# First stage of a two-layer diffusion block: small vectors as columns, band means by token tile, pool weights amid conditioning

## The chip, the cores and the metric

The kernel runs on one core of a Trainium2 chip, in one launch. The metric is the time of the device for one execution, in microseconds, as the median of the runs of one kernel. A profile of a single execution goes with it: its span runs from the first to the last instruction. Engine names in the profile: PE is TensorE's matmuls, PEld its weight loads, DVE is VectorE, ACT is ScalarE, POOL is GpSimd, SP is SyncE, which issues the loads and stores (DMA).

## The reference

Two layers run over 512 latent tokens and 256 context tokens of width 1024, all in float32. Layer 0 mixes tokens by pooling, layer 1 by attention; each is followed by a squared-ReLU MLP. What matters here is the start of layer 0:

```python
sh1, sc1, gt1, sh2, sc2, gt2 = ada_mods(c, w_ada[i], b_ada[i])       # silu(c) @ w + b, six vectors of 1024
csh1, csc1, cgt1, csh2, csc2, cgt2 = ada_mods(c_ctx, w_ada[i], b_ada[i])
h_lat = modulate(rms_norm(x, g_mix_pre[i]), sh1, sc1)                # h * (1 + scale) + shift
y_lat = pool_mixer(h_lat, w_pool[j], pool_scale[j])                  # per group of 256 channels:
                                                                     # (mean over 2, 4, 8 or 16 tokens - h) @ w_pool[g]
x = x + gt1 * rms_norm(y_lat, g_mix_post[i])
m_lat = sq_relu_mlp(modulate(rms_norm(x, g_mlp_pre[i]), sh2, sc2), w_mlp_in[i], w_mlp_out[i])
x = x + gt2 * rms_norm(m_lat, g_mlp_post[i])
```

The context goes the same way with its own vectors. The output is the latent stream after both layers.

## The kernel before

**Tiling.** Tokens come in six tiles of 128 (`NL` = 4 latent, then 2 context, `NT` = 6), channels in eight tiles of 128 (`KT` = 8, index k). A weight matmul in full precision is made of three in the format float32r (high by high, high by low, low by high), for which weights and activations are split: a cast on ACT (`split`, L128) and a subtraction on DVE (L131). The matmuls of the bands, the conditioning, the gate rows and the transposes take plain float32; each of them shows as two instructions in the profile.

**Order.** The work of a stage is put into a list of steps, each with a time that serves as a rank (`st.at(t, fn, ...)`, class `Steps`), and is emitted in the order of these ranks. A planner then places the emitted instructions on the engines by its own timeline: what is ready by that timeline may go ahead of what was emitted earlier. Only instructions marked with `keep_in_program_order` stay as emitted; the loads of `raw_load` are such. All loads and stores are issued by SP in one queue.

**First stage** (steps at L713 to L751). Its parts, with the lines that the profile names:

- Small vectors (L185 to L214). `b_ada`, the gains, `c` and `c_ctx` are loaded as rows of 128 into two work tiles `pr1` and `pr2`, between the loads of x; two transposes on TensorE (L208, L209) turn them into columns in the PSUM tile `pp`. From there come the conditioning input `cond` (SiLU on ACT, L211), `cols` (L213) and `gpc` (L214).
- x (`xload`, L191). Six loads of 512 KB, the pooling bands (`band`) after the third.
- `rows_a`, `rows_b`. Per token tile: square and sum on ACT (L156), two small operations on POOL (L163, L171), scaling on DVE into `acc` (L332).
- Bands. Pooling is a matmul of the token tile with a band matrix of 144 columns; `bands` is made from the loaded one by four copies on DVE (L401, L402). `mean_mm(k, narrow)` (L420) does all six token tiles of one channel tile into a PSUM buffer (`psm`): of the pool `psA`, which has two buffers of two banks, or, for k = 4 and 7, two of `psB`, which has four of one bank. For k = 0 and 1 `mean_ev` (L434) moves the result to `stage` in SBUF.
- Conditioning (`ada_mm`, `ada_sel`). Fourteen blocks in the order of `CONDITIONING` (scale and shift before the mixer, gate, scale and shift before the MLP), twenty loads of 1 MB through a ring of four buffers (`rawe`). Each load takes matmuls (L226), a block then a DVE transpose (L228), small matmuls (L233) and one to three small DVE operations (L244 to L253). The buffer of a load comes free when these have read it.
- `centred(k)` applies scale and shift to the means of channel tile k and splits the result: three operations on ACT (L452, L455) and three on DVE (L454, L456).
- `pool_weights`. One load through the same ring, the pool scale as a broadcast load, a product on DVE (L469), then the split on ACT and DVE.
- `pool_a(t)` (L480) is the pool matmul of a token tile, 24 instructions into one buffer of `psA`. It needs every `centred` and the pool weights. Then come its mean square on ACT, the gate (`gate_rows`, L302 and L304, out of the seventh and eighth conditioning blocks), residual, norm, transposes (`turn0`, L378), modulation (`mod0`) and the first products of the MLP (`part`, L553), tile pair by tile pair.

The rank lines that the change touches are these:

```python
    landing = (21, 26.3, 29, 32, 39, 42, 47.3, 52.6, 61, 66, 69, 72, 74.8, 77.7)
    for z, (m, j, w) in zip(landing, CONDITIONING):
        ada_at(st, z, 0, m, j, w)
    for k in range(KT):
        st.at([15, 16, 18, 20, 22, 29.5, 31, 35][k], mean_mm, k, k in (4, 7))
        if k < 2:
            st.at(16.5 + k, mean_ev, k, (True, False))
        st.at([27.5, 28.5, 29.6, 30.6, 33.2, 34.2, 43.2, 44.2][k], centred, k)
    st.at(33.5, pool_weights)
```

After the first stage the MLP of layer 0, attention and the MLP of layer 1 follow, with their own steps; the first matmul of the next block is L553 with the tile `units`.

## Time and profile before

| | |
|---|---|
| median of 3 runs | 1178.87 us (1178.73 to 1179.42) |
| profiled execution | 1180.54 us, span 1178.7 us |
| PE busy | 1142.6 us, 97% |
| DVE busy | 941.9 us, 80% |
| ACT busy | 637.5 us, 54% |
| first stage | 0 to 109.9 us |

A row of the timeline gives start and duration in us, engine, line, operation, the tiles written and read, the shape and the count, and in brackets the idle time ahead of it with what ended it. A row of the table by stretches gives busy time and instructions of each engine, then the clock granted to TensorE, the busy share of the DMA engines and their rate. A row of groups gives the count, the busy time in us, the mean of one in ns, and the idle time ahead with what ended it. DMA issues are listed with the size and the time from issue to landing.

### The profile page before, as it was taken

What the parts mean: (1) busy time and instruction counts of PE and PEld (TensorE: products, weight loads), DVE (VectorE), ACT (ScalarE), POOL (GpSimd) and SP (SyncE); (2) the same over time, 40 slices, a digit from 0 to 9 for tenths busy, and PEclk for the clock granted to TensorE, in tenths of its full rate; (3) what the DMA queues carried; (4) which work ended last, traced back from release to release, by engine and by line L of the source; (5) the groups of instructions that cost most, each with busy time, mean ns of one, the idle gap of its engine ahead of it and who ended that gap; (6) DMA issues with size and microseconds to landing.
All of it is one profiled execution on the core that took longest, in us unless ns stands there. A gap on an engine that the chain in (4) does not pass through costs nothing.

```text
span 1178.7 us, 15984 instructions
## 1 busy us (share of the span) xinstructions
PE 1142.6 (97%) x6170; PEld 989.5 (84%) x6170; DVE 941.9 (80%) x1546; ACT 637.5 (54%) x1087; POOL 67.2 (6%) x120
## 2 busy tenths in 40 slices
PE   5899999999999999999999999999899999999997
PEld 4679888989889988998887889998888888888886
DVE  3786778998988999896787689877687779778876
ACT  3666654555354445554676377863676346535522
POOL 2030000000000000000141210001100000000001
PEclk9899999999999999999999999999999999999999
DMA  8974222333334334334422101115234124304312
GB/s 325 369 290 196 72 72 107 143 143 144 143 143 142 113 139 143 107 132 151 182 72 75 70 1 36 37 43 199 110 119 174 48 97 142 108 36 143 107 38 105
DMA packets 25642, 147.84 MB, mean 125 GB/s; under 512 B 2736, under 2 KB 5216, under 8 KB 9824
## 3 DMA queue, kind: packets, MB, share of 16 engines
q1 hardware_dynamic: 25568, 146.84, 34.1%
q8 instruction: 48, 0.79, 0.3%
q14 instruction: 26, 0.21, 0.1%
HBM read 139.49 MB, written 7.34 MB: 125 GB/s over the span
## 4 chain that ended last, share of the span: by engine, by line
PE 54%; issue 33%; DVE 5%; ACT 3%; POOL 3%; DMA 1%; SPq 0%; POOLq 0%; DVEq 0%; ACTq 0%
PE pso L771 22%; PE psin L677 18%; PE psin L553 3%; PE po L1230 2%; PE psy L1256 2%; PE psq L1018 2%; PE pss L1191 2%; POOL rs L171 1%; PE psada L226 1%; PE psm L420 1%; POOL rs L1027 1%; ACT junk L156 1%; DVE sm L1195 1%; PE pspt L1216 1%; DVE units L1219 1%
## 5 line engine op out<-in xcount | busy, mean ns | idle before, releaser
L771 PE MATMUL pso<-units,rb 128*128 128x512 f32 x1152 | 278.9, 392 | 0.0
L771 PEld LDWEIGHTS pso<-units,rb 128*128 128x128 f32 x1152 | 214.7, 188 | 41.1
L268 DVE SCALAR_TENSOR_TENSOR rows<-raw,cond,rows 128x256 f32<-128x256 f32 x280 | 127.1, 479 | 2.0
L783 DVE TENSOR_TENSOR acc<-acc,pso 128x512 f32<-128x512 f32 x129 | 85.4, 677 | 41.8 <-PE pso L771 41.7
L553 PE MATMUL psin<-ra,rb 128*128 128x512 f32 (+1 forms) x432 | 104.8, 342 | 2.4 <-ACT ra L363 1.6
L875 PE MATMUL pso<-units,pairs 128*128 128x512 f32 x336 | 82.3, 389 | 0.0
L553 PEld LDWEIGHTS psin<-ra,rb 128*128 128x128 f32 x432 | 70.3, 189 | 13.7 <-ACT ra L363 1.9
L553 PE MATMUL psin<-ra 128*128 128x512 f32 x256 | 80.5, 389 | 0.0
L875 PEld LDWEIGHTS pso<-units,pairs 128*128 128x128 f32 x336 | 63.1, 188 | 13.1
L879 DVE TENSOR_TENSOR acc<-acc,pso 128x512 f32<-128x512 f32 x72 | 48.8, 683 | 28.6 <-PE pso L875 28.6
L169 POOL TENSOR_SCALAR ms<-ss 128x1 f32<-128x1 f32 x20 | 11.0, 549 | 1000.7 <-ACT junk L156 989.2
L677 PE MATMUL psin<-ra,units 128*128 128x384 f32 x336 | 65.5, 337 | 0.4 <-ACT psin L689 0.4
L677 PE MATMUL psin<-sums,units 128*128 128x384 f32 x336 | 64.0, 336 | 0.0
L677 PEld LDWEIGHTS psin<-ra,units 128*128 128x128 f32 x336 | 59.8, 188 | 3.9 <-ACT psin L689 0.5
L131 DVE TENSOR_TENSOR units<-raw,units 128x1024 fp32r<-128x1024 f32 (+2 forms) x49 | 55.2, 1153 | 6.5 <-ACT units L128 6.3
L677 PEld LDWEIGHTS psin<-sums,units 128*128 128x128 f32 x336 | 58.9, 188 | 1.6
L128 ACT CAST units<-raw 128x1024 fp32r<-128x1024 f32 (+2 forms) x49 | 46.9, 995 | 17.7 <-PE pso L771 13.7
L553 PEld LDWEIGHTS psin<-ra 128*128 128x128 f32 x256 | 48.1, 188 | 10.0
L781 ACT COPY acc<-pso 128x512 f32<-128x512 f32 x48 | 27.1, 587 | 48.2 <-PE pso L771 47.7
L553 PE MATMUL psin<-rb 128*128 128x512 f32 (+1 forms) x144 | 52.8, 367 | 0.2 <-DVE rb L364 0.2
L1018 PE MATMUL psq<-units,ra 128*128 128x512 f32 x216 | 51.7, 392 | 0.0
L553 PE MATMUL psin<-rb,ra 128*128 128x512 f32 x128 | 49.8, 389 | 0.0
(255 smaller groups left out, 2355.7 us busy)
## 6 DMA issues: line engine op xcount, KB each, us to landing
raw<-in_w_ada SPq DMA_DIRECT2D x48, 1024.0 KB, 4.9
raw<-in_w_mlp_in SPq DMA_DIRECT2D x32, 1024.0 KB, 4.8
raw<-in_w_mlp_out SPq DMA_DIRECT2D x32, 1024.0 KB, 5.0
raw<-in_w_qkv SPq DMA_DIRECT2D x6, 1024.0 KB, 4.8
spill<-xr SPq DMA_DIRECT2D x10, 512.0 KB, 9.1
xr<-spill SPq DMA_DIRECT2D x10, 512.0 KB, 5.6
raw<-in_w_o SPq DMA_DIRECT2D x4, 1024.0 KB, 4.9
xr<-in_x SPq DMA_DIRECT2D x4, 512.0 KB, 4.4
```

Of the source, the lines that this page charges most:

```text
L128: a = sc.copy(hi, raw)
L131: b = ve.tensor_tensor(out=lo, in0=raw, in1=hi, op=ALU.subtract)
L268: ve.scalar_tensor_tensor(out=r, in0=raw[:, k, :], scalar=cond[:, k, c:c + 1], in1=r, op0=ALU.mult, op1=ALU.add)
L553: te.matmul(ps[:, bank, o:o + ln], w[:, k, fs], rhs, start=start, stop=(k == KT - 1 and n == 2), skip_group_check=len(ks) < KT)
L677: te.matmul(bank, w[k], a[k], start=start and k == 0 and m == 0, stop=stop and k == 3 and m == 2, skip_group_check=True)
L771: te.matmul(pss[h][:, 0:cols[h][1]], a[:, f, ts_], w[:, f, cols[h][0]:sum(cols[h])], start=(n == 0 and not seeded[t]), stop=(n == len(seq) ...
L781: sc.copy(d, ps)
L783: ve.tensor_tensor(out=d, in0=d, in1=ps[:, 0:w], op=ALU.add)
L875: te.matmul(ps, a, w, start=(m == 0), stop=(m == len(seq) - 1))
L879: ve.tensor_tensor(out=M[n][:, t], in0=M[n][:, t], in1=ps, op=ALU.add)
L1018: te.matmul(ps, a[:, k, sl], w[:, k % 4, :], start=(k == 0 and n == 0), stop=(k == KT - 1 and n == 2))
L1191: te.matmul(ps[:, c2, 0:384], a[:, sl], b[:, kv, 384 * c2:384 * c2 + 384], start=(n == 0), stop=(n == 2))
```

## The change

The host packs the small vectors as columns into one array `vecs` of 128 by 176; two loads ahead of x bring them in, the seven loads of rows, the two transposes and the copies from PSUM go. SiLU reads its input from `phase`. The bands' load follows the first tile of x. Bands are worked by token tile: `band_open` takes the PSUM buffers of a pair of channel tiles (latent means in `psA`, context means of both in one buffer of `psB`), `band_mm(t, ks)` does one token tile for several channel tiles, `band_ev` moves the pairs of k = 0 and k = 2 to `stage`. The first four channel tiles are done as the token tiles come, the others later, one k at a time. The pool weights are loaded after the fourth conditioning load (step 21.5; before, after the sixth, step 33.5). The ranks of the other steps of this stage are moved, the first block's load of MLP weights behind one more conditioning block.

```diff
@@ -79,8 +78,8 @@
 
     acc = const.tile([P, NT * D], F32, name="acc")
     ident = const.tile([P, P], F32, name="ident")
-    cols = const.tile([P, 128], F32, name="cols")
-    gpc = const.tile([P, 32], F32, name="gpc")
+    vec = const.tile([P, 160], F32, name="vec")
+    cols, gpc = vec[:, 0:128], vec[:, 128:160]
     cond = const.tile([P, KT, 32], F32, name="cond")
     sel = const.tile([P, 32], F32, name="sel")
     mods = [const.tile([P, 48, 2], F32, name=f"mods{i}") for i in range(2)]
@@ -182,36 +181,19 @@
     ve.memset(cond, 0.0)
     ve.tensor_scalar(out=onesr, in0=ident[:, 0:2], scalar1=0.0, scalar2=1.0, op0=ALU.mult, op1=ALU.add)
 
-    pr1 = work_tile()[:, 0:P]
-    pr2 = work_tile()[:, 0:P]
-    ve.memset(pr2, 0.0)
-    row = lambda a: a.rearrange("l (r p) -> (l r) p", p=P)
+    given = phase[:, 16:32]
+    sy.dma_start(given, vecs[:, 160:176])
+    sy.dma_start(vec, vecs[:, 0:160])
     xt = x.rearrange("b (t p) d -> p (b t) d", p=P)
     ct = ctx_in.rearrange("b (t p) d -> p (b t) d", p=P)
     xload = lambda t: sy.dma_start(xr[:, t, :], xt[:, t, :] if t < NL else ct[:, t - NL, :])
     xload(0)
-    sy.dma_start(pr2[32:40, :], row(c))
-    sy.dma_start(pr2[40:48, :], c_ctx.rearrange("(r p) -> r p", p=P))
-    xload(1)
-    sy.dma_start(pr2[0:16, :], row(g_mix_post))
-    sy.dma_start(pr2[16:32, :], row(g_mlp_post))
-    xload(2)
     sy.dma_start(gate.rearrange("p a n -> p (a n)")[:, 8 * BW:12 * BW + 64], band)
-    xload(3)
-    sy.dma_start(pr1[0:96, :], row(b_ada))
-    sy.dma_start(pr1[96:112, :], row(g_mix_pre))
-    xload(4)
-    sy.dma_start(pr1[112:128, :], row(g_mlp_pre))
-    xload(5)
-
-    pp = psB.tile([P, 512], F32, tag="b", name="pp")
-    te.transpose(pp[:, 128:256], pr2, ident)
-    te.transpose(pp[:, 0:128], pr1, ident)
+    for t in range(1, NT):
+        xload(t)
+    sc.activation(cond[:, :, 0:2].rearrange("p k c -> p c k"), given.rearrange("p (c k) -> p c k", k=KT),
+                  AF.Silu)
     ve.tensor_reduce(out=sel, in_=ident.rearrange("p (j c) -> p c j", c=32), axis=AX.X, op=ALU.add)
-    sc.activation(cond[:, :, 0:2].rearrange("p k c -> p c k"),
-                  pp[:, 160:176].rearrange("p (c k) -> p c k", k=KT), AF.Silu)
-    ve.tensor_copy(cols, pp[:, 0:128])
-    ve.tensor_copy(gpc, pp[:, 128:160])
 
     rowsd, parts, seeded, stale = {}, {}, {}, [0]
 
@@ -401,38 +383,33 @@
         ve.tensor_copy(bands[:, v], bands[:, 2])
         ve.tensor_copy(bands[:, v, :, c:c + HALO], edges[:, v])
 
-    means = {}
-
-    def mean_mm(k, narrow):
-        g = k // 2
-        if narrow:
-            ps = [psB.tile([P, 512], F32, tag="b", name="psm") for _ in range(2)]
-        else:
-            both = psA.tile([P, 2, 512], F32, tag="a", name="psm")
-            ps = [both[:, q, :] for q in range(2)]
-        means[k] = ps
-        for q, n in ((0, NL), (1, NT - NL)):
-            for i in range(n):
-                v = 0 if i == 0 else (1 if i == n - 1 else 2)
-                lo = max(i * P - HALO, 0)
-                hi = min((i + 1) * P + HALO, n * P)
-                c0 = lo - (i * P - HALO)
-                te.matmul(ps[q][:, lo:hi], accv[:, q * NL + i, k * P:(k + 1) * P],
-                          bands[:, v, g, c0:c0 + hi - lo], start=(i == 0), stop=(i == n - 1),
-                          skip_group_check=True)
-
-    stage = []
-
-    def mean_ev(k, on_act):
-        if len(stage) % 2 == 0:
-            stage.append(rawp.tile([P, 2048], F32, tag="raw", name="stage"))
-            d = stage[-1][:, 0:TOK]
-        else:
-            stage.append(stage[-1])
-            d = stage[-1][:, TOK:2 * TOK]
-        for (t0, ln), ps, a in zip(SEGS, means[k], on_act):
-            (sc.copy if a else ve.tensor_copy)(d[:, t0:t0 + ln], ps[:, 0:ln])
-        means[k] = [d[:, t0:t0 + ln] for t0, ln in SEGS]
+    means, lat, con = {}, {}, {}
+
+    def band_open(k):
+        lat[k] = psA.tile([P, 2, 512], F32, tag="a", name="psm")
+        con[k] = psB.tile([P, 2, 256], F32, tag="b", name="psc")
+        for u in range(2):
+            means[k + u] = lat[k][:, u, :], con[k][:, u, :]
+
+    def band_mm(t, ks):
+        q, i, n = (0, t, NL) if t < NL else (1, t - NL, NT - NL)
+        v = 0 if i == 0 else (1 if i == n - 1 else 2)
+        lo, hi = max(i * P - HALO, 0), min((i + 1) * P + HALO, n * P)
+        c0 = lo - (i * P - HALO)
+        for k in ks:
+            te.matmul(means[k][q][:, lo:hi], accv[:, t, k * P:(k + 1) * P], bands[:, v, k // 2, c0:c0 + hi - lo],
+                      start=(i == 0 and (q == 0 or k % 2 == 0)), stop=(i == n - 1), skip_group_check=True)
+
+    stage = {}
+
+    def band_ev(k, q, on_act):
+        if k not in stage:
+            stage[k] = rawp.tile([P, 2048], F32, tag="raw", name="stage")[:, 0:2 * TOK].rearrange("p (u n) -> p u n", n=TOK)
+        t0, ln = SEGS[q]
+        (sc.copy if on_act else ve.tensor_copy)(stage[k][:, :, t0:t0 + ln], (lat, con)[q][k])
+        if q:
+            for u in range(2):
+                means[k + u] = [stage[k][:, u, t0:t0 + ln] for t0, ln in SEGS]
 
     rs, mix, yg, first = {}, {}, {}, []
 
@@ -712,41 +689,51 @@
 
     st = Steps()
     for t in range(NT):
-        st.at([2.965, 5.5, 6.559, 8.059, 9.559, 12.094][t], rows_a, t)
-        st.at([5.159, 8.462, 12.185, 11.882, 11.6, 13.1][t], rows_b, t)
-    landing = (21, 26.3, 29, 32, 39, 42, 47.3, 52.6, 61, 66, 69, 72, 74.8, 77.7)
+        st.at(4.6 + 1.3 * t, rows_a, t)
+        st.at(6.8 + 1.3 * t, rows_b, t)
+    landing = (15.3, 20.3, 26.2, 28.6, 31, 33.4, 39.5, 44.3, 49, 53.5, 58.5, 61, 63.4, 65.8)
     for z, (m, j, w) in zip(landing, CONDITIONING):
         ada_at(st, z, 0, m, j, w)
+    for k in (0, 2):
+        st.at(7.9, band_open, k)
+    for t in range(NT):
+        st.at(8 + 1.3 * t, band_mm, t, range(4))
+    for q, z in ((0, 13.2), (1, 15.8)):
+        for k in (0, 2):
+            st.at(z, band_ev, k, q, (k == 0) == (q == 0))
+    for k in range(4, KT):
+        z = 16.5 + 2.6 * (k - 4)
+        if k % 2 == 0:
+            st.at(z - 0.1, band_open, k)
+        for t in range(NT):
+            st.at(z + t / 10, band_mm, t, (k,))
     for k in range(KT):
-        st.at([15, 16, 18, 20, 22, 29.5, 31, 35][k], mean_mm, k, k in (4, 7))
-        if k < 2:
-            st.at(16.5 + k, mean_ev, k, (True, False))
-        st.at([27.5, 28.5, 29.6, 30.6, 33.2, 34.2, 43.2, 44.2][k], centred, k)
-    st.at(33.5, pool_weights)
-    st.at(36.5, lambda: split(*pw[0]))
+        st.at([22, 23.5, 25, 26.5, 30.2, 31.7, 35, 36.2][k], centred, k)
+    st.at(21.5, pool_weights)
+    st.at(27.5, lambda: split(*pw[0]))
     raws = []
-    st.at(55, lambda: first.append(Inner(0, w_in(0, 0, ring, False, raws), hH, hL, hids0[0], chunks0, TOK)))
-    st.at(59, lambda: split(*raws[0]))
+    st.at(55.5, lambda: first.append(Inner(0, w_in(0, 0, ring, False, raws), hH, hL, hids0[0], chunks0, TOK)))
+    st.at(57, lambda: split(*raws[0]))
     for h in range(2):
         for ci in range(2):
-            st.at((48.5, 54)[h] + (0.1, 0)[ci], gate_rows, 0, GT1, ci, (h,))
+            st.at((40.9, 45.7)[h] + (0.1, 0)[ci], gate_rows, 0, GT1, ci, (h,))
     order = (4, 5, 0, 1, 2, 3)
     for n, t in enumerate(order):
-        b = 55 + 3 * n
-        st.at((45.3, 48.7, 55.5, 58.5, 61.5, 64.5)[n], pool_a, t)
-        st.at(max(b - 0.5, 50 + n), pool_ms, t)
+        b = 46.4 + 3 * n
+        st.at((36.4, 39.8, 46.8, 49.8, 52.8, 55.8)[n], pool_a, t)
+        st.at(max(b - 0.5, 41 + n), pool_ms, t)
         st.at(b, pool_b, t)
         st.at(b + 1.5, norm_r, t)
         st.at(b + 2.8, norm_s, t)
         st.at(b + 4, norm_c, t, n % 2 == 1)
     parts0 = lambda t, q, f: first[0].part(t, f, range(2 * q, 2 * q + 2))
-    block = {(4, 0): 66.5, (4, 1): 68, (0, 0): 69.5, (0, 1): 71, (4, 2): 72.7, (0, 2): 74, (2, 0): 75.3, (2, 1): 76.6,
-             (2, 2): 77.9, (4, 3): 79.2, (0, 3): 80.4, (2, 3): 81.6}
+    block = {(4, 0): 54.7, (4, 1): 56.2, (0, 0): 60.4, (0, 1): 61.7, (4, 2): 63, (0, 2): 64.3, (2, 0): 66.6, (2, 1): 67.8,
+             (2, 2): 69, (4, 3): 70.3, (0, 3): 71.5, (2, 3): 72.7}
     for (t, q), z in block.items():
         st.at(z, turn0, t, q)
         st.at(z + 0.8, mod0, t, q)
         for f in range(2):
-            st.at(z + 2.4 if q < 3 else 83 + 2 * f + t / 10, parts0, t, q, f)
+            st.at(z + 2.4 if q < 3 else 74.2 + 2 * f + t / 10, parts0, t, q, f)
     st.at(200, open_units)
     st.run()
 
@@ -1333,8 +1320,8 @@
     mlp1(first1[0], last1)
 
 
-_INS = ["x", "c", "ctx", "c_ctx", "w_ada", "b_ada", "g_mix_pre", "g_mix_post", "g_mlp_pre", "g_mlp_post",
-        "w_pool", "pool_scale", "w_qkv", "g_q", "g_k", "w_o", "w_mlp_in", "w_mlp_out"]
+_INS = ["x", "ctx", "w_ada", "w_pool", "pool_scale", "w_qkv", "g_q", "g_k", "w_o", "w_mlp_in", "w_mlp_out"]
+_VECS = ["b_ada", "g_mix_pre", "g_mlp_pre", "g_mix_post", "g_mlp_post", "c", "c_ctx"]
 
 
 def _blocks(w, width):
@@ -1361,6 +1348,7 @@
     out["w_mlp_out"] = np.stack([_blocks(w, D)[0] for w in out["w_mlp_out"]])
     for n in ("w_qkv", "w_o"):
         out[n] = _blocks(out[n][0], 512)
+    out["vecs"] = np.concatenate([inputs[n].reshape(-1, P) for n in _VECS]).T
     return {f"in_{n}": np.ascontiguousarray(a) for n, a in out.items()}
 
 
```

5 lines of the change are left out of this document (2 added, 3 removed).

## The prediction

> **What bounds the kernel now.** I read the page first, then a table by stretches that I cut at the events of the first stage.
>
> ```profile
> span 1178.7 us, 15984 instructions
> PE 1142.6 (97%) x6170; PEld 989.5 (84%) x6170; DVE 941.9 (80%) x1546; ACT 637.5 (54%) x1087; POOL 67.2 (6%) x120
> ```
> ```profile
> core 0: us, PE busy (x) PEld busy (x) DVE busy (x) ACT busy (x) POOL busy (x), PEclk, DMA share, GB/s
> 0.00:9.78 9.78, 0.45 (x2) 0.19 (x2) 3.24 (x10) 5.02 (x9) 3.50 (x12) 1.00 0.80 284
> 9.78:21.86 12.08, 9.47 (x36) 6.84 (x37) 4.25 (x9) 5.79 (x10) 2.65 (x7) 1.00 1.01 401
> 21.86:30.08 8.22, 7.42 (x84) 5.28 (x86) 1.99 (x7) 0.00 (x1) 0.00 (x0) 1.00 0.73 255
> 30.08:53.57 23.49, 19.43 (x186) 13.96 (x178) 19.64 (x40) 15.96 (x25) 0.00 (x0) 0.85 0.93 360
> 32.10:38.93 6.83, 6.03 (x40) 4.85 (x41) 6.21 (x14) 5.09 (x10) 0.00 (x0) 0.50 1.02 429
> 53.57:109.90 56.33, 53.47 (x505) 43.26 (x505) 41.07 (x73) 37.40 (x73) 13.76 (x24) 1.00 0.72 277
> 109.90:1178.70 1068.80, 1052.35 (x5370) 920.01 (x5368) 871.71 (x1409) 573.31 (x972) 47.32 (x78) 1.00 0.30 107
> ```
>
> TensorE is the bound of the whole: it is idle 36.1 of 1178.7 us. The last row says that 16.45 us of this idle time lie in the 1068.8 us after the first stage, which the edit does not touch. The stage that it does touch ends at 109.90, when the first MLP block's matmuls (L553) are through. Inside it the limits differ. Up to 9.78 TensorE has nothing to do. From 30.08 (the first `centred` starts) to 53.57 (the last one ends) VectorE is busy 19.64 of 23.49 us and TensorE does short pieces between. From 53.57 to 109.90 TensorE is idle only 2.86 us, so that part is a fixed sum of matmul work: what starts it earlier ends the stage earlier.
>
> TensorE's own rows tell how the early time is used (start, duration, idle before in brackets):
>
> ```profile
> 9.78 3.19 PE L420 MATMUL psm<-gate,acc 128*128 128x136 f32 x12 [2.55 <-DVE gate L402]
> 17.97 1.27 PE L420 MATMUL psm<-gate,acc 128*128 128x136 f32 x4 [0.42 <-DVE acc L332]
> 19.18 1.94 PE L226 MATMUL psada<-raw,cond 128*32 128x512 f32 x8
> 21.05 4.90 PE L420 MATMUL psm<-gate,acc 128*128 128x136 f32 x36
> 25.88 2.78 PE L226 MATMUL psada<-raw,cond 128*32 128x512 f32 x24
> 32.90 3.14 PE L420 MATMUL psm<-gate,acc 128*128 128x136 f32 x12 [2.21 <-DVE work L454]
> 53.74 1.22 PE L480 MATMUL pspool<-rb,ra 128*128 128x256 f32 x8
> 54.80 1.95 PE L302 MATMUL psg<-ident,gc 128*128 128x128 f32 x16
> 56.67 1.92 PE L226 MATMUL psada<-raw,cond 128*32 128x512 f32 x16
> ```
>
> A band matmul (L420) is two instructions, and these cost 0.27 us each in the first row, 0.136 in the run of 36. The conditioning matmuls (L226) say the same, 0.24 each at 19.18 and 0.116 at 25.88: TensorE ran at half clock until about 21, though the clock column prints 1.00 there. It lost the clock once more from 32.10 to 38.93 (0.50). The planner already runs the bands of k=0 and 1 tile by tile (the twelve of the first row need the first three tiles). Those of k=2 and 3 come only in the 36 from 21.05, ahead of the three conditioning loads that follow at 25.88 and on which the first `centred` waits.
>
> The input side, from the queue and the tile `raw`:
>
> ```profile
> xr<-in_x SPq DMA_DIRECT2D x4, 512.0 KB, 4.4
> gate<-in_band SPq DMA_DIRECT2D x1, 320.0 KB, 4.6
> raw<-in_w_ada SPq DMA_DIRECT2D x20, 1024.0 KB, 7.9
> 0.72 0.85 SPq L191 DMA_DIRECT2D xr<-in_x  x2
> 7.69 0.42 SPq L191 DMA_DIRECT2D xr<-in_ctx  x1
> DMA to landing us min/median/max: 6.0/6.0/6.0
> L109 SPq DMA_DIRECT2D raw<-in_w_ada x4: 328/431/647, 8.2 to 10.0; - x4
> DMA to landing us min/median/max: 8.0/10.8/13.7
> 5.00:10.00 5.00, 0.67 (x2) 0.41 (x3) 2.33 (x5) 3.21 (x7) 3.03 (x6) 1.00 0.99 360
> 10.00:15.00 5.00, 4.09 (x17) 3.69 (x17) 1.59 (x3) 3.33 (x6) 1.64 (x5) 1.00 1.01 372
> 15.00:20.00 5.00, 3.30 (x12) 2.11 (x16) 2.29 (x6) 2.24 (x5) 0.79 (x2) 1.00 1.00 423
> ```
>
> The last token tile lands at 7.7 + 6.0 = 13.7. The first four conditioning loads, issued from 8.2 to 10.0, land from 16.2 to 23.7 (10.0 + 13.7), 2.5 us apiece. The engines of the queue are full throughout (0.99 to 1.01), but they move 360 and 372 GB/s while the small vectors are mixed in, 423 after.
>
> **The change, part by part.**
>
> *Vectors as columns.* Seven small loads, two transposes, two copies and a clear give way to two loads ahead of x. Two issues cost about 0.85 us by the queue's first row, so the first tile lands 0.9 later, at 5.3 for 4.4. The shortfall of 63 and 51 GB/s over two stretches of 5 us is 0.57 MB, 1.35 us at 423. At 423 from 5.3 on, the five other tiles and the bands (2.95 MB) land by 12.3, the four loads (4.19 MB more) at 14.8, 17.2, 19.7 and 22.2: 1.4 us earlier than now. Bounds: nothing gained, or 2 us. The Trainium skill, "DMA: Bandwidth & Descriptors", Measured, speaks against this edit: transfers under 64 KB are limited by their descriptors, and it gives 0.68 us for 4 KB and 0.95 for 64 KB, for loads issued by another engine than here. By that the two loads would hold up x by about 1.7 us instead of 0.9, an estimate, and the gain would shrink by up to 0.8. The rows speak mildly for the rule, since the rate falls with small loads in the stream.
>
> *SiLU ahead of the rows.* Its input now comes first, so the table load moves out of ScalarE's row work:
>
> ```profile
> 4.45 1.06 ACT L156 ACTIVATE junk<-xr 128x1024 bf16<-128x1024 f32 x1 [2.24 <-DMA xr<-in_x]
> 6.60 0.75 DVE L332 TENSOR_SCALAR acc<-xr,rs 128x1024 f32<-128x1024 f32 x1 [4.84 <-POOL rs L171]
> 13.65 1.28 ACT L211 ACT_TABLE_LOAD   x1
> 30.08 1.52 ACT L452 ACTIVATE work<-stage,mods,avec 128x512 f32<-128x512 f32 x2 [10.17 <-DVE mods L244]
> ```
>
> A tile's way from landing to scaled row is 4.45 to 7.35, 2.9 us. The last tile takes 4.2 now (13.7 to 17.9) because 1.28 us of table load stand ahead of its square; it will be ready at 12.3 + 2.9 = 15.2. The cover for the table load is ScalarE's wait for the first tile; if that cover fails it costs 1.3.
>
> *Four channel tiles of bands as x lands.* The bands' load moves from the eighth place in the queue to the fourth, so the 2.55 us wait on `gate` goes and TensorE starts at 8.2. Each tile then has 8 instructions: 2.1 us at half clock, 1.1 at full, against a new tile every 1.25. At half clock throughout, the six tiles end at 21.2; at full clock at 16.4, one tile's work after the last row. I take 17.4: half clock for the first two tiles and a half, to about 13.6, full for the rest, because TensorE now works without a pause from 8.2, and in the trace it gained its clock some 3 us into its first unbroken run (17.97 to about 21).
>
> *First `centred`.* After 17.4 come the four loads, about 1.0 us each, and by the order of the steps k=4 and 5 between them, 24 instructions at 0.136, 3.3 us: 24.7. From the last conditioning matmul (28.66) to `centred` (30.08) takes 1.4, and the scaling of the pool weights may stand 2.3 us in VectorE's way. I take 27.0 where it is 30.08; bounds 25.5 and 29.
>
> *`centred` and pool weights.* The work stays, and its engines are these:
>
> ```profile
> L456 DVE SCALAR_TENSOR_TENSOR ra<-work,mods,ra 128x256 fp32r<-128x256 f32 (+1 forms) x16 | 9.2, 604 | 0.6 <-ACT ra L455 0.5
> L131 DVE TENSOR_TENSOR rb<-raw,rb 128x2048 fp32r<-128x2048 f32 x1 | 2.3, 2293 | 1.2 <-ACT rb L128 1.2
> L469 DVE TENSOR_TENSOR raw<-raw,pscale 128x2048 f32<-128x2048 f32 x1 | 2.3, 2284 | 0.0
> L455 ACT ACTIVATE ra<-work,phase 128x256 fp32r<-128x256 f32 (+1 forms) x16 | 8.7, 608 | 0.5 <-DVE work L454 0.5
> ```
>
> Loaded fifth instead of seventh, the pool weights' 4.6 us on VectorE no longer hold the last channel tiles, and the later conditioning lands at 2.5 us steps: the pool weights and their scale by 26, the eight conditioning loads done by 36. So the 3.85 us of idle VectorE in this stretch can close. VectorE needs 19.64 from 27.0: 46.6, and I take 47.0. ScalarE needs 15.96 and ends earlier. Bounds: 44.5 if the scaling runs ahead of 27, 50.5 if all idle time stays.
>
> *The rest of the stage.* At 53.57 TensorE has 53.47 us ahead of it. Of that, the first gate rows (1.95) and the last two gate loads (1.92, landing by 46) can now run before 47.0. On the other side about 30 pool matmuls are left instead of 8 (the second tile's accumulator comes free only with the last `centred`): 22 at 0.13, 2.8. With today's idle 2.86 that is 53.47 - 1.95 - 1.92 + 2.8 + 2.9 = 55.3, and the stage ends at 102.3 where it ends at 109.9.
>
> **Sum: 7.6 us.** After the stage, TensorE is 98.5% busy and everything is shifted alike, so it is kept. The profiled execution took 1180.54 with a span of 1178.7; its sum gives a span of 1171.1. The median of the runs shown, 1178.87, stands 0.2 above the span, so the forecast is 1171.3. A difference of 0.2%, 2.4 us, is about what a measurement can tell from none.
>
> **Rivals.**
>
> *The clock does not hold.* If the bands run at half clock to the end (21.2 for 17.4), 3.8 us of the gain go: 1175.1. TensorE will also be under half busy between about 28 and 39, waiting for loads; a thinly used stretch, with a pause of 2.21 us at its end (the row at 32.90), is what stands around 32.10 in the trace. A second 6.83 us at half clock costs 3.4, if the pool matmuls fall into it: 1174.7. Against it: much of that work waits on VectorE anyway. The Trainium skill, "TensorE: Matmul & The Clock Gate", Part 1, ties the loss to an idle window of about 3.4 us; by that rule loads 2.5 us apart would keep the clock and nothing would be lost. The trace does not bear it out: the pause was 2.21 us, and the clock was gone before it ended. A half gain also comes if the ring of four load buffers stalls: the pool weights hold one of them from landing until they are split, some 12 us.
>
> *More than forecast.* If VectorE's work closes up to 44.5 and TensorE's 2.86 us of idle time vanish, the stage ends at 97: 1166. Not much speaks for a stage without any waits.
>
> *Slower: the order of all that follows.* The steps are only a wish; the planner places instructions by its own clock, and a shift of the start can swap instructions later. Those 1068.8 us hold 16.45 us of idle time now. From 26.5 us on (2.5% instead of 1.5%) the kernel would be over 0.2% slower; with one percent more idle and half the gain, 1186. For it: the places of the later steps have three decimals and suit one order. Against it: loads and engines shift together, and the order there is set by TensorE's queue, which does not care when it starts.
>
> *The edit does not do what it says.* The planner interleaves by tile already, and could put the new steps back to where they were, with the stage set by VectorE and buffers as now: within 0.2%.
>
> **How the numbers follow.** Forecast (6 to 11 us gained) 0.50; a half gain, by clock or ring, 0.24; more than 11 us 0.08; no change 0.07; slower 0.11. Faster is the sum of the first three, 0.82. The range leaves out the slower case and part of no change at the top and the extreme of more at the bottom: 1167 to 1177.5.
>
> **What would show it.** Right: TensorE's first L420 near 8.2, 48 of these instructions done by 17 to 18, the first `centred` near 27, the last one near 47, the first matmul of the next block (L553 with `units`) near 102. Wrong: band instructions still at 0.27 us after 15, `centred` not before 29, or, with all of these right, more than 17 us of idle TensorE behind the stage.

## The result, and the profile after

The change makes no difference that can be measured: 1179.50 us median of 14 runs against 1179.43 of 14 runs of the kernel before, ratio 1.0003 [0.9995, 1.0012]. The forecast was 1171.3 (1167.0 to 1177.5).

The profiled execution took 1181.59, with a span of 1179.80; executions of this kernel spanned 1176.9 (mean granted clock 0.994) to 1183.3 (0.991). So differences of a microsecond or two between two profiles are not the kernels', and verdicts below go by the ratios.

The lines have moved: L400 is the bands, L208 the conditioning matmuls, L215 the small ones, L226 the `mods`, L446 the product of the pool weights, L130 the subtraction of a split, L457 the pool matmuls, L284 the gate rows. The table by stretches of the changed kernel:

```profile
core 0: us, PE busy (x) PEld busy (x) DVE busy (x) ACT busy (x) POOL busy (x), PEclk, DMA share, GB/s
8.63:28.64 20.01, 19.70 (x136) 14.57 (x136) 6.65 (x11) 6.23 (x11) 5.82 (x10) 1.00 0.97 370
30.04:53.17 23.13, 15.89 (x156) 9.67 (x159) 19.59 (x40) 15.71 (x25) 0.00 (x0) 0.78 0.98 360
33.24:36.66 3.42, 2.83 (x28) 1.21 (x32) 3.42 (x8) 3.42 (x6) 0.00 (x0) 0.50 1.00 402
40.07:46.90 6.83, 6.01 (x50) 3.84 (x50) 5.20 (x14) 3.46 (x6) 0.00 (x0) 0.50 0.96 360
53.17:111.08 57.91, 54.90 (x505) 44.95 (x505) 40.92 (x72) 36.83 (x73) 14.13 (x24) 0.97 0.71 263
60.55:63.96 3.41, 3.41 (x20) 3.01 (x22) 1.36 (x3) 0.85 (x2) 0.00 (x0) 0.50 1.02 394
111.08:1179.80 1068.72, 1052.50 (x5370) 919.93 (x5368) 871.20 (x1409) 575.15 (x972) 47.19 (x78) 1.00 0.30 107
```

The last row answers the rival of a slower order behind the stage: there TensorE takes 1068.72 us with 16.22 idle, where it was 1068.80 with 16.45. What differs lies in the first stage. TensorE is 98% busy there from 8.63 to 28.64 (19.70 of 20.01), and three stretches at half clock follow where there was one. TensorE's rows show with what it was busy, and VectorE's what the first channel tiles waited for:

```profile
8.63 6.11 PE L400 MATMUL psm<-gate,acc 128*128 128x136 f32 x32 [8.63 <-DVE acc L314]
15.03 1.19 PE L400 MATMUL psc<-gate,acc 128*128 128x136 f32 x8 [0.30 <-DVE acc L314]
16.06 3.02 PE L400 MATMUL psm<-gate,acc 128*128 128x136 f32 x24
19.02 1.05 PE L208 MATMUL psada<-raw,cond 128*32 128x512 f32 x2
19.99 1.19 PE L400 MATMUL psc<-gate,acc 128*128 128x136 f32 x8
21.11 1.06 PE L208 MATMUL psada<-raw,cond 128*32 128x512 f32 x6
22.10 1.19 PE L400 MATMUL psc<-gate,acc 128*128 128x136 f32 x8
...
24.22 1.22 PE L400 MATMUL psm<-gate,acc 128*128 128x136 f32 x8
25.38 1.06 PE L208 MATMUL psada<-raw,cond 128*32 128x512 f32 x8
26.37 1.19 PE L400 MATMUL psc<-gate,acc 128*128 128x136 f32 x8
...
27.58 1.05 PE L208 MATMUL psada<-raw,cond 128*32 128x512 f32 x8
29.46 0.25 PE L215 MATMUL psada<-raw,sel 128*32 128x8 f32 x8 [0.84 <-DVE raw L210]
33.29 1.93 PE L208 MATMUL psada<-raw,cond 128*32 128x256 f32 x16 [3.57 <-DMA raw<-in_w_ada]
...
40.89 0.29 PE L215 MATMUL psada<-rows,sel 128*32 128x4 f32 x8 [3.42 <-DVE mods L226]
```
```profile
14.89 1.21 DVE L409 COPY stage<-psm 128x1024 f32<-128x1024 f32 x1
16.03 0.74 DVE L314 TENSOR_SCALAR acc<-xr,rs 128x1024 f32<-128x1024 f32 x1
20.76 0.69 DVE L409 COPY stage<-psc 128x512 f32<-128x512 f32 x1 [3.99 <-PE psc L400]
```

All 96 band instructions, k=4 to 7 too, stand ahead of or among the first four conditioning loads. The first of these landed at 15.02 and is not done before 22.2, the last landed at 22.47 and is done at 28.6. The later channel tiles went ahead of the first four as well. The latent means of these (32 instructions) are through at 14.7. Their last token tile is scaled only at 16.77, behind a copy to `stage` on VectorE; by then 24 latent instructions of later channel tiles are in TensorE's queue (16.06), its own eight follow at 19.99, and the copy at 20.76 waited 3.99 us for them.

So the first `centred` starts at 30.04, as before (30.08). The buffers come free as late: the pool weights are issued at 22.23 and land at 29.96, and the fifth conditioning load lands at 33.15, for which TensorE waits 3.57.

The stage can be counted from these rows. Its end is TensorE's busy time plus its idle time, and work in a stretch with 0.50 in the clock column takes about twice as long (16 conditioning matmuls of 256 columns: 1.93 us at 33.29, 1.07 at 82.68). The first `centred`, the first gate vector (`mods` of the seventh block), the next block's first matmul, and TensorE's busy and idle time before that, all in one profile each, us. The half clock at the start, where the column prints 1.00, is not counted in the column for it:

| kernel | first `centred` | gate vector | next block | busy | idle | busy at half clock | ratio to before |
|---|---|---|---|---|---|---|---|
| before | 30.1 | 54.0 | 109.9 | 90.2 | 19.7 | 6.0 | 1 |
| after | 30.0 | 53.6 | 111.1 | 90.7 | 20.3 | 12.2 | 1.0003 |
| e1 columns only | 28.8 | 54.2 | 109.7 | 89.1 | 20.6 | 3.4 | 1.0008 [0.9999, 1.0017] |
| e2 conditioning first | 25.7 | 50.2 | 106.1 | 85.8 | 20.3 | 2.7 | 0.9974 [0.9965, 0.9984] |
| e3 pool late | 30.7 | 56.6 | 112.5 | 88.9 | 23.6 | 7.0 | 1.0019 [1.0006, 1.0031] |
| e4 = e2 + e3 | 26.8 | 52.5 | 108.8 | 88.0 | 20.9 | 7.2 | 0.9977 [0.9968, 0.9986] |
| e5 = e2 + small first | 25.5 | 49.3 | 105.3 | 84.7 | 20.7 | 3.4 | 0.9977 [0.9969, 0.9986] |
| e6 = e2 + late product | 25.7 | 53.0 | 111.2 | 87.0 | 24.2 | 5.7 | 1.0018 [1.0007, 1.0029] |
| e7 = e5 + late product | 25.7 | 51.7 | 110.7 | 89.5 | 21.2 | 12.5 | 1.0007 [0.9998, 1.0016] |
| e8 before, conditioning first | 26.2 | 51.0 | 107.2 | 87.5 | 19.7 | 3.4 | 0.9989 [0.9980, 0.9997] |
| e9 = e2 + pool first | 32.0 | 56.2 | 113.5 | 91.7 | 21.8 | 12.2 | 1.0010 [1.0001, 1.0019] |
| e10 = e5 + pool first | 33.1 | 51.1 | 108.3 | 87.3 | 21.0 | 7.7 | 1.0013 [1.0004, 1.0021] |
| e11 = e2 + GpSimd | 25.8 | 52.7 | 106.8 | 87.4 | 19.4 | 4.6 | 0.9991 [0.9982, 1.0000] |
| e12 = e5 + product later | 25.7 | 51.4 | 112.0 | 88.8 | 23.2 | 12.0 | 1.0013 [1.0003, 1.0023] |
| e13 = e2 + product later | 25.6 | 52.2 | 106.5 | 86.5 | 20.0 | 5.8 | 0.9996 [0.9986, 1.0005] |
| e14 after + extra bands | 30.4 | 53.5 | 110.8 | 93.4 | 17.4 | 6.8 | 1.0008 [1.0000, 1.0017] |
| e15 = e5 + extra bands | 25.6 | 49.5 | 107.3 | 89.1 | 18.2 | 0 | 1.0003 [0.9994, 1.0012] |
| e16 = e12 + extra bands | 26.2 | 48.9 | 105.2 | 88.7 | 16.5 | 0 | 0.9987 [0.9977, 0.9996] |
| e17 = e5 + pool third | 32.6 | 51.1 | 108.4 | 86.7 | 21.7 | 4.9 | 1.0004 [0.9995, 1.0013] |

The stage is read from one execution, the ratio from all. The profiled executions of the changed kernel, e9 and e12 took 2.1 to 2.9 us more than the median of their kernel, those of e2, e5, e16 and e17 1.0 to 2.5 less. Between these two groups a difference in the stage can be too large by 3 us and more. e9 and e10, for one, are 5.2 us apart in the stage and not apart in the ratio.

### The profile page after: what moved, and what is told of

The parts are those of the page before. It is cut to its first block, busy times and chain, and to the rows that moved or that the text cites. A ratio compares the mean times of both kernels' runs of the same rounds, so it can differ in the third digit from the quotient of the medians.

```text
span 1179.8 us, 15965 instructions
## 1 busy us (share of the span) xinstructions
PE 1143.2 (97%) x6168; PEld 989.3 (84%) x6168; DVE 941.9 (80%) x1543; ACT 639.2 (54%) x1087; POOL 68.9 (6%) x120
## 4 chain that ended last, share of the span: by engine, by line
PE 49%; issue 42%; DVE 3%; POOL 3%; ACT 2%; DMA 1%; SPq 0%; POOLq 0%; DVEq 0%; ACTq 0%
PE pso L758 22%; PE psin L654 18%; PE psin L530 3%; PE psq L1005 2%; PE pspool L457 2%; PE psada L208 1%; POOL rs L170 1%; ACT junk L155 1%; POOL rs L1014 1%; DMA xr<-in_x 1%; DVE xr L310 0%; PE psc L400 0%; PE psx L360 0%; DVE rows L250 0%; DVE ra L433 0%
## 5 line engine op out<-in xcount | busy, mean ns | idle before, releaser
L758 PEld LDWEIGHTS pso<-units,rb 128*128 128x128 f32 x1152 | 214.8, 188 | 41.2
L130 DVE TENSOR_TENSOR units<-raw,units 128x1024 fp32r<-128x1024 f32 (+2 forms) x49 | 55.2, 1149 | 5.0 <-ACT units L127 4.9
L768 ACT COPY acc<-pso 128x512 f32<-128x512 f32 x48 | 27.1, 587 | 50.0 <-PE pso L758 49.6
L1005 PE MATMUL psq<-units,ra 128*128 128x512 f32 x216 | 51.7, 392 | 0.0
```

The lines of the kernel that those rows point to most:

```text
L130: b = ve.tensor_tensor(out=lo, in0=raw, in1=hi, op=ALU.subtract)
L758: te.matmul(pss[h][:, 0:cols[h][1]], a[:, f, ts_], w[:, f, cols[h][0]:sum(cols[h])], start=(n == 0 and not seeded[t]), stop=(n == len(seq) ...
L768: sc.copy(d, ps)
L1005: te.matmul(ps, a[:, k, sl], w[:, k % 4, :], start=(k == 0 and n == 0), stop=(k == KT - 1 and n == 2))
```

## The experiments

**e1: the columns alone.** The kernel before with the host's `vecs`, its two loads, SiLU from `phase`, and the loads in the order of the change; bands and ranks as before.

> The kernel before with the vectors as columns alone; bands, pool weights and ranks as before. Theory 1 (the data comes earlier, the gain is lost on TensorE, which in the changed kernel works off all band matmuls before the four conditioning loads): here TensorE keeps the old order, only three channel tiles' bands stand ahead of the second to fourth load, so the first centred comes about 2 us earlier than 30.1 and the kernel takes 1177 to 1178. Theory 2 (the gain is lost later, where pool weights and the two single-channel-pair blocks meet on VectorE): first centred earlier all the same, but the last one ends near 53 and the time is 1179. Theory 3 (what follows the last centred takes up any slack): 1179 too, with the last centred early.

The conditioning loads land 0.6 to 0.7 earlier (15.5 to 23.0), the first `centred` comes 1.3 earlier and the last one ends at 51.7 instead of 53.6. The time does not follow. TensorE's and VectorE's rows show where the 1.9 us go:

```profile
50.75 1.07 PE L208 MATMUL psada<-raw,cond 128*32 128x512 f32 x8
51.75 2.05 PE L462 MATMUL pspool<-rb,ra 128*128 128x256 f32 x15
53.73 0.25 PE L215 MATMUL psada<-raw,sel 128*32 128x8 f32 x8
```
```profile
51.88 0.72 DVE L210 STREAM_TRANSPOSE raw<-psada 128x512 f32<-128x512 f32 x1 [0.22 <-PE psada L208]
54.05 0.17 DVE L226 TENSOR_TENSOR mods<-psada,vec 128x8 f32<-128x8 f32 x1 [1.45 <-PE psada L215]
```

The gate block's second load has landed by 48.5; its matmuls stand behind 15 pool matmuls (from 48.77) until 50.75. The transpose is done at 52.6, the small matmuls stand behind 15 more until 53.73, and the gate vector comes at 54.2 (54.0 before). Here the rest of the stage follows the gate vector and not the last `centred`: the one is 0.2 us later than before, the other 1.9 earlier, the next block 0.2 earlier. That is nearest to the third theory. That it is so in every kernel is not shown: over the 19 profiles the next block starts 54.1 to 60.6 us after the gate vector, and 55.6 to 61.9 after the last `centred`, which does not tell the two apart.

**e2: conditioning ahead of the later bands.** In the changed kernel the first instructions of the bands of k=4 to 7 are held in place.

```diff
+            z = te.matmul(...)
+            if k > 3 and t in (0, NL):
+                tc.keep_in_program_order(z)
...
-        z = 16.5 + 2.6 * (k - 4)
+        z = (19, 21.4, 21.41, 21.42)[k - 4]
...
-            st.at(z + t / 10, band_mm, t, (k,))
+            st.at(z + t / 1000, band_mm, t, (k,))
```

> The changed kernel with the bands of channel tiles 4 to 7 queued behind the conditioning: tile 4 behind the scale block, tiles 5 to 7 behind the shift block. Theory 1: the fourth load's matmuls end near 23.7 instead of 28.6, the first centred starts near 25.2 instead of 30.0, the buffers come free 4 to 5 us earlier, and the kernel takes 1174 to 1175. Theory 2: the first centred starts near 25 but the last one still ends within 2 us of 53, and the time is 1177.5 to 1179.5. Theory 3: the last centred ends near 48 and the time is nevertheless 1178 to 1179.5.

Faster than both kernels, by 0.26% than the one before; with e4 and e5 (0.23%) it is the best of all that ran. TensorE's rows:

```profile
16.46 1.07 PE L208 MATMUL psada<-raw,cond 128*32 128x512 f32 x8
17.58 1.20 PE L400 MATMUL psc<-gate,acc 128*128 128x136 f32 x8
18.70 1.07 PE L208 MATMUL psada<-raw,cond 128*32 128x512 f32 x8
...
22.40 1.92 PE L208 MATMUL psada<-raw,cond 128*32 128x512 f32 x16
25.16 0.25 PE L215 MATMUL psada<-raw,sel 128*32 128x8 f32 x8 [0.84 <-DVE raw L210]
```

The four loads are through by 24.3 instead of 28.6, and the stage is 5.0 us shorter in these two profiles; by the ratios e2 is 0.29%, or 3.4 us, ahead of the changed kernel. The 1174 to 1175 of the first theory are not reached (median 1177.55). The stretch from the first `centred` to the last, in the table by stretches, is no shorter than before:

```profile
25.70:49.73 24.03, 17.33 (x192) 12.29 (x191) 19.52 (x40) 16.04 (x25) 0.00 (x0) 0.93 0.99 389
```

**e8: the same on the kernel before.** The first instruction of the bands of k=2 to 4 is held, their ranks become 22.5, 27.4 and 27.45.

> The kernel before with the first of these edits alone: the bands of channel tiles 2 to 4 queued behind the conditioning blocks, all else as it was. If the gain of e2 is that of the order and not of the edit under study, this has most of it too: the fourth load's matmuls end near 25 instead of 28.7, the first centred starts near 26.5, and the time is 1176 to 1178. If it takes the early data and the bands by token tile to use that order, the time is that of the kernel before within 1 us.

First `centred` 26.2 for 30.1, next block 107.2 for 109.9: the order helps without what the change adds. The ratio shows less than the profile, 0.1%. In this profile 1.5 us are given back behind the stage, with a stretch at half clock at 844 us.

**e3, e4: pool weights as late as before** (`pool_weights` at 29.7, its split at 34.5), on the changed kernel and on e2.

> The changed kernel with the pool weights back behind the sixth conditioning load and their split behind centred 5. Theory 1: the first centred stays at 30, and the time within 1 us of the changed kernel's, 1179. Theory 2: the fifth conditioning load lands near 30 instead of 33, its scale and shift are not held by the 2.3 us subtraction of the pool weights, centred 4 starts near 37 instead of 41.5, the last one ends near 49, and the kernel takes about 1176.

> Both edits together. Theory 1: as with the conditioning first alone, 1174 to 1175. Theory 2: only both together give the forecast's order; first centred near 25, the last one ends near 46 to 47, the time 1172 to 1173. Theory 3: 1178 to 1179.5 whatever the last centred does.

On the changed kernel the early place is worth 0.16%, with intervals that overlap; with the conditioning first no difference can be measured. What holds back the conditioning is the bands, wherever the pool weights stand.

**e5, e6, e7: what holds the 24 us.** e5 holds the first matmul of each group of `pool_a` for the context tiles and moves the second `pool_a` from 39.8 to 40.6, so that L215 comes ahead. e6 loads the pool weights seventh and holds their product behind the fifth block's `mods` (rank 32.3) and their split behind that. e7 does both.

> The kernel with the conditioning first (e2), and the pool matmuls of the first two token tiles queued behind the small conditioning matmuls of the shift block and of the first gate block. Theory 1 (TensorE's order holds the conditioning up: in e2 the small matmuls at 43.55, 44.87 and 49.70 each stand behind 10, 8 and 22 pool matmuls): the last scale and shift vectors are ready near 43.5 instead of 45.3, the first gate vector near 47 instead of 50.2, and as the next block has followed that vector by 55.5 to 57.5 us in every run so far, it starts near 103 and the kernel takes about 1175. Theory 2 (VectorE holds it, the pool weights' 4.6 us and 2.3 us of waiting for them): nothing moves, 1177.5, or up to 1 us more because pool matmuls start later.

> The kernel with the conditioning first (e2), the pool weights loaded seventh, and their two operations on VectorE queued behind centred 5 and behind the last shift block. Theory 1: VectorE's order does not matter, 1177 to 1178. Theory 2: VectorE works off centred 0 to 3 without the pause from 26.8 to 29.1, the vectors of the third pair of blocks are ready near 34 instead of 39, centred 4 starts near 34.5 instead of 39.5, the last one ends near 46 instead of 49.7; the pool matmuls start later, near 43; the kernel takes 1174 to 1176.

> All three edits: bands, pool matmuls and pool weights queued behind the conditioning. If both engines' orders hold the conditioning up, this is the forecast's order: last centred ends near 46, first gate vector near 46 to 47, next block near 102 to 103, 1172 to 1174. If the stage's tail does not follow, 1177.

e5: the first gate vector comes 0.9 earlier, the second 0.2 later, the time is that of e2. e6: the `mods` of the third and fourth block come at 33.9 and 34.7 instead of 38.9 and 39.4, as meant, and the stage is 5 us longer. TensorE's rows:

```profile
46.80 5.77 PE L464 MATMUL pspool<-rb,ra 128*128 128x256 f32 x46 [0.59 <-DVE rb L130]
52.50 0.25 PE L215 MATMUL psada<-raw,sel 128*32 128x8 f32 x8
```

The pool matmuls now wait for the split until 46.7, and the gate block's small ones stand behind 46 of them. The gate vector is 2.8 us later; the rest of the 5 lies behind it, and its cause was not traced. e7 takes these away from there, but has 17.1 us at half clock from 34.0.

**e9, e10, e17: pool weights ahead of `centred`.** `pool_weights` at 15 (first of the ring) on e2 and on e5, or at 16 (third) on e5, split held at 17, so that VectorE does both operations before the first `centred`.

> The kernel after the change, with the bands of k=4 to 7 held behind the conditioning as in the run with the conditioning first, and the pool weights and their scale loaded ahead of the first conditioning block, multiplied and split on VectorE while it is idle (it had 7.8 us of work between 8.8 and 25.7 there). Theory (VectorE between the first and the last `centred` sets the rest: of the 24.0 us there, 2.3 are its wait for the pool weights and 4.5 its work on them): the fourth conditioning load waits for the pool weights' buffer and the first `centred` comes at 28.3 instead of 25.7, but the stretch behind it shrinks by 6.8 to 17.2, the last `centred` ends at 45.5, the first gate vector is there at 46, the next block at 102, span 1170.5, ratio 0.994. Rival (clock: with less to do TensorE falls to half clock in the stretch and behind it): next block 104, span 1172.7, ratio 0.996. Rival (TensorE and the landings set that stretch, VectorE only fills it): it stays 24 us long, the last `centred` ends at 52.3, next block 108.5, span 1177.2, ratio 1.000.

> The run with the pool weights first, and the pool matmuls of the two context tiles held in place, so that the small conditioning matmuls (`sel`) do not stand behind them. Theory (VectorE): as without this edit, within 1 us of span, since the first gate vector came 0.9 us earlier with it and the second no earlier: next block 101 to 102, span 1170, ratio 0.994. Rival (the place of the small matmuls decides once VectorE is relieved): the gate vectors come 2 us earlier than without it and the span is 2 us shorter.

> The run with the conditioning first and the small matmuls ahead, with the pool weights and their scale loaded between the first and the second conditioning block, so that VectorE multiplies and splits them before the first `centred`. Theory (what the run with the pool weights first and the small matmuls ahead showed: 18.4 us from the first `centred` to the last, because VectorE has 14.8 us there and not 19.5, but a first `centred` at 33.1): the first `centred` comes at 29.5 to 30.5, since the second block's loads land 4 us later, the first gate vector at 47.5 to 48.5 and not at 49.3, the next block at 103.5 to 104.5, ratio 0.996. Rival (the sum is conserved: what VectorE gains, the later landings take): first gate vector at 49 to 51, next block 105 to 107, ratio 0.9975 to 0.999. Rival (clock: TensorE, thinly used from 19 to 30, drops to half clock before the first `centred`): first `centred` at 31 or later, next block 106 to 108, ratio 1.000.

The stretches from the first `centred` to the last, of e9 and of e10:

```profile
32.00:55.00 23.00, 19.02 (x192) 13.52 (x190) 15.00 (x38) 13.91 (x24) 0.00 (x0) 0.85 0.92 360
```
```profile
33.10:51.50 18.40, 15.05 (x189) 11.15 (x188) 14.79 (x41) 13.88 (x24) 0.00 (x0) 1.00 0.96 386
```

In e9 VectorE has 4.5 us less to do and the stretch is 1 us shorter than in e2: its work alone does not set it, though e9 has 6.8 us at half clock in it and e2 3.4. In e10 the stretch is 5.6 us shorter than in e2, at full clock and with the small matmuls ahead, and in e17 as short (18.4). But in e9 and e10 the 1.5 MB of weights and scale ahead of the conditioning move the first `centred` to 32 and 33. e17 pays the same price, by the wait for its second block and half clock from 28.2:

```profile
26.86 1.07 PE L208 MATMUL psada<-raw,cond 128*32 128x512 f32 x8 [3.99 <-DMA raw<-in_w_ada]
29.25 1.94 PE L208 MATMUL psada<-raw,cond 128*32 128x512 f32 x8 [1.32 <-DMA raw<-in_w_ada]
```

Of e17's three outcomes the last is the nearest: first `centred` at 32.6, next block at 108.4, ratio 1.0004.

**e11: the product on GpSimd** (`gp.tensor_tensor` in place of `ve.tensor_tensor`, on e2). The expectation speaks of the subtraction as well; in the kernel that ran it stayed on VectorE.

> The run with the conditioning first, pool weights loaded where the change loads them, but their product and the subtraction of their split done on GpSimd, which has nothing to do in that stretch. Theory (VectorE): the first `centred` stays at 25.7, VectorE loses 4.5 us of work and 2.3 us of waiting, the last `centred` ends between 43 and 46, the next block is at 100 to 102, span 1169.5 to 1171, ratio 0.993 to 0.994, if GpSimd does both operations before 45, which leaves it 14 us for what takes VectorE 4.5. Rival (GpSimd is more than three times as slow): the pool matmuls wait for the low halves of the weights, and the next block slips by as much behind 102 as they end behind 45. Rival (TensorE and the landings set the stretch): last `centred` 49, next block 106, span 1174.5, as without the edit.

VectorE's and GpSimd's rows, and the same four VectorE instructions in e6:

```profile
28.45 6.22 DVE L435 SCALAR_TENSOR_TENSOR ra<-work,mods,ra 128x256 fp32r<-128x256 f32 x4 [1.59 <-ACT ra L434]
```
```profile
28.55 4.78 POOL L448 TENSOR_TENSOR raw<-raw,pscale 128x2048 f32<-128x2048 f32 x1 [12.54 <-DMA raw<-in_w_pool]
```
```profile
28.39 2.16 DVE L435 SCALAR_TENSOR_TENSOR ra<-work,mods,ra 128x256 fp32r<-128x256 f32 x4 [1.58 <-ACT ra L434]
```

While GpSimd multiplies, VectorE's four instructions take 6.22 us for 2.16: it stood still for 4.1 of GpSimd's 4.78, more than the 2.29 that the product costs on VectorE itself. The next block comes at 106.8 (106.1 in e2), not at 100 to 102.

**e12, e13: the product in between.** The product held at 26.6, behind three `centred`, the split held at 30.3, the load left fifth; e12 on e5, e13 on e2.

> The kernel after the change with the bands of k=4 to 7 behind the conditioning, the pool weights loaded where the change loads them, their product placed on VectorE behind the low halves of the first three `centred`, the subtraction of their split behind the mods of the third and fourth conditioning blocks, and the small conditioning matmuls ahead of the pool matmuls. Theory (the order on VectorE holds back the last channel tiles): VectorE's wait of 2.3 us for the pool weights is gone, the mods of the third and fourth block come at 36 instead of 38.9, those of the fifth and sixth at 41 instead of 45.3, the last `centred` ends at 46.5, the first gate vector (its loads land at 44.0) comes at 47, the next block at 103, span 1171.7, ratio 0.995. Rival (the landings: the buffer of the pool weights comes free later, so the gate loads land 2 to 4 us later): the first gate vector at 49 to 50, next block 105 to 106, span 1174 to 1174.7, as with the bands alone. Rival (clock: a second stretch at half clock falls into the pool matmuls): next block 104.5 with the mods as in the theory.

> The same without holding the small conditioning matmuls ahead of the pool matmuls. Theory (VectorE's order): the mods of the third to sixth block as in the run with it, the first gate vector 1 to 2 us later, since its small matmuls stand among pool matmuls; next block 104 to 105, span 1173, ratio 0.996. Rival (landings): same span as with it, within 0.5 us.

The `mods` of the third and fourth block come at 36.6 and 37.5, near the 36 expected; those of the fifth and sixth at 45.0 and 45.8, no earlier than in e2 (44.2 and 45.3): the split now stands ahead of them, at 41.2, and TensorE is at half clock from 35.8 to 42.6. That VectorE's order alone holds the stage is not borne out; with the clock held (e16 below) the same order has the last two `mods` at 39.2 and 43.4. e13 is 0.17% ahead of e12, with intervals that overlap, although its gate vector comes 0.8 later; why e12 takes the longest of all behind that vector (60.6) is not shown.

**e14, e15, e16: the clock.** Latent bands of k=6 and 7 are computed again into the same buffers while TensorE waits; e14 on the changed kernel (27.1 and 29.5 alone), e15 on e5, e16 on e12 (28.7 with k=6 and 7 in place of 29.5). The lines of e15:

```diff
...
+    def again(*ks):
+        for k in ks:
+            for t in range(NL):
+                band_mm(t, (k,), True)
...
+    for z, ks in ((22.1, (6,)), (27.1, (7,)), (29.5, (6, 7, 6))):
+        st.at(z, again, *ks)
```

> The changed kernel, with the latent bands of k=6 and 7 computed again into the same buffers (32 extra instructions, 4.4 us at 0.137) while TensorE waits: once after the third conditioning block's matmuls, three times after the fourth's. Before that TensorE runs as in the changed kernel. Theory (the clock: 12.2 of the 90.7 us that TensorE was busy in this stage fell into stretches at half clock, 6.1 us lost, against 1.4 in the run with the conditioning first): the first stretch from 33.2 stays, since TensorE is idle from 29.7 to 33.3 as before, but the one from 40.1 to 46.9 goes, with at least 3 of its 3.4 us; the next block is at 107 to 108.5 and the ratio 0.9975. Rival (the stretches at half clock fall into waiting, VectorE and the landings set the stage): the clock holds, but the next block stays at 111 and the ratio at 1.000. Rival (the extra work does not hold the clock): the stretch at 40 stays and the kernel is 0 to 2 us longer.

> The run with the conditioning first and the small conditioning matmuls held ahead, with the same extra bands in TensorE's waits: once before the third conditioning block, once behind it, three times behind the fourth (40 instructions, 5.5 us). Theory (clock): the one stretch at half clock from 38.8 to 42.2 goes, 1.7 us: next block 103.6 to 104, span 1172.5 to 1173, ratio 0.996. Rival (waiting): next block 105.3 and span 1174.2 as without.

> The run with the pool product behind the first `centred` and the small matmuls ahead, with extra bands of k=6 and 7 in TensorE's waits: once before the third conditioning block, once behind it, twice behind the fourth (32 instructions, 4.4 us). Without them 12.0 us of TensorE's work there fell into half clock (stretches from 35.8, 46.0 and 107.5), 6 us lost. Theory (clock): the stretches go, the mods of the fifth and sixth block come at 42 to 43 instead of 45 to 45.8, the first gate vector at 47 to 48 instead of 51.4, the next block at 103.5 to 106, ratio 0.996 to 0.998. Rival (VectorE's order): mods at 45, next block 109 to 112.

e14, from the table by stretches and TensorE's rows:

```profile
40.07:46.90 6.83, 6.83 (x91) 4.58 (x90) 5.76 (x18) 3.47 (x6) 0.00 (x0) 1.00 0.95 360
```
```profile
48.63 1.06 PE L208 MATMUL psada<-raw,cond 128*32 128x512 f32 x8 [1.17 <-DMA raw<-in_w_ada]
```

The clock holds and the gate vector does not move (53.5 for 53.6): the second load of the gate block, the tenth of all, lands at 48.6, and its small matmuls stand behind 22 pool matmuls, as in the changed kernel. This stretch of half clock filled waits. e16 is the opposite: with the clock held for the whole stretch (in the profiled execution, mean granted clock 0.999; over all eleven it was 0.995 to 0.999) the gate vector comes 2.5 us earlier and the next block 6.9, the ratio falls from 1.0013 to 0.9987.

```profile
26.20:48.90 22.70, 19.76 (x217) 14.60 (x217) 19.25 (x41) 15.84 (x25) 0.00 (x0) 1.00 0.99 394
```

e15 holds the clock too, and loses 0.26% against e5: the gate vector stays at 49.5, the next block comes 57.8 us behind it instead of 56.0. The extra work changed the order behind; the price of the clock cannot be read from e15. Nor are e16's 6.9 us that price alone. They are nearly all idle time (23.2 to 16.5), 4.4 of them lie behind the gate vector, where the extra work changed TensorE's order too, and by the ratios e16 gains 0.26%, 3.1 us.

## Why the prediction was wrong

*Columns and SiLU* came true. The first tile landed at 5.33 (5.3), the last at 12.54 (12.3), the four loads at 15.0, 17.5, 20.0 and 22.5 (14.8 to 22.2). That the first tile lost only the 0.9 of two issues was in part luck of this profile: in the 17 profiles with the two loads ahead it landed between 5.26 (e5) and 6.12 (e17), 0.8 to 1.7 later than the 4.43 before. The Trainium skill's figure for small loads ("DMA: Bandwidth & Descriptors", Measured), by which x would have lost 1.7 us (an estimate), is the upper end of that. SiLU's table load (1.28 us from 2.57) ended before the first tile landed.

*Four channel tiles of bands as x lands* came true only at its start. The bands started at 8.63 (8.2) and were at half clock until about 12.8 (13.6). The last token tile was scaled at 16.8, not 15.2, and the first four channel tiles were done at 21.2, not 17.4. The 48th band instruction does end at 17.2, as the sign asked, but by then eight of the 48 are of later channel tiles.

*First `centred`* is the step that failed. "By the order of the steps k=4 and 5 between them" took the ranks for the order, though the text says elsewhere that the planner places what is ready by its own timeline. It put all four remaining channel tiles first, 48 instructions and not 24: half of them ahead of the last token tile of the first four and of every load, the others between the loads. Each load's matmuls waited. The first `centred` came at 30.04, outside the bounds of 25.5 to 29. With only k=4 ahead of the fourth load (e2) it was 25.7.

*`centred` and pool weights* failed on its own account. Even with the order right, first to last `centred` takes 24.0 us where 20.0 were taken, and the last one ends at 49.7, not 47.0; eight conditioning loads are in at 39.0 (e2) and 40.9 (after), not 36. VectorE's idle time was counted as slack that closes. It is part of a ring: a load needs a buffer, its matmuls need TensorE, the `mods` need VectorE, and these free the buffer and the PSUM tile for the next (up to 112 us the queue of the changed kernel waits 30.2 us for conditioning matmuls to free a buffer; TensorE waits 3.4 for the `mods` ahead of 40.89). In the changed kernel the product and the split of the pool weights stand in that ring on VectorE:

```profile
31.03 2.28 DVE L446 TENSOR_TENSOR raw<-raw,pscale 128x2048 f32<-128x2048 f32 x1
...
37.13 2.29 DVE L130 TENSOR_TENSOR rb<-raw,rb 128x2048 fp32r<-128x2048 f32 x1
...
40.76 0.12 DVE L226 TENSOR_TENSOR mods<-psada,vec 128x4 f32<-128x4 f32 x1
```

The fifth load's `mods` come 7.6 us after its landing. But each way of taking one link away (VectorE's order in e6, e12 and e13, its work in e9, the clock in e14) was followed by another wait, so no single one sets the 24 us. e10 and e17 alone shortened the stretch much, to 18.4, with VectorE's pool work ahead of it and the small matmuls held, and both start it 7 us later than e2. What would shorten it without that stays open.

*The rest of the stage* was mis-sized: 55.3 us from the last `centred`, measured 57.9 (56.3 in e2), of which some 1.7 is the half clock from 60.55 (an estimate: half of 3.41). The gate rows and the second gate block could not run ahead of the last `centred`, since the gate vector comes after it (53.6 and 53.2; in e2 50.2 and 49.7).

*The rivals.* A slower order of all that follows: not seen (1068.72 us for 1068.80). The clock: the half-clock work doubled, to 12.2 us from 6.0 before the change, and the difference of e2 to the changed kernel in TensorE's busy time (4.9 us) is nearly all half clock (4.8); but e14, which held the second of the three stretches, gained nothing, so that one only filled waits. The first and the third were not held, and whether they did too stays open. So it is shown that the order of the bands costs the kernel 0.29%, but not how much of this is the later `centred` and how much the half clock that the order brings with it; TensorE's idle time is the same in both (20.3). "The planner could put the new steps back to where they were" had 0.07 and was the nearest. It moved them the other way.

## What to carry over

Where a planner places instructions, a rank is a wish: before a moved step is costed, ask for each engine what is ready earlier and would be put ahead of the step that the path waits for. Work that is off the path (here bands needed only at 40) must be held behind the loads' consumers, since these also free the buffers of the loads to come. And a stage that runs in a ring of buffers does not give back an engine's idle time when one wait is closed; look for the vector or tile on which the tail really hangs.
